# Attention values kept in rows of 4 KB and loaded earlier, with queries and keys ahead of them, more products ahead and more buffers

## The chip, the cores and the metric

One Trainium2 chip, one of its cores. The metric is the device time of one execution in microseconds (us); before the change the median of three runs is 1877.93 us (1871.57 to 1879.18).

## What is computed

One layer of a hybrid encoder on 1024 tokens of width 1024, in float32. Only branch A matters here:

```python
p = h @ w_in                       # h: normed, modulated x; q, k, v are 1024 columns each
q, k = rmsnorm(q, g_q), rmsnorm(k, g_k)      # per head, 16 heads of 64
z = q @ k.T / 8                    # strictly causal: s < t
log_a = log_sigmoid(z) + (exclusive suffix sum of log_sigmoid(-z))
y_a = (exp(log_a), 0 where s >= t) @ v
merged = sigmoid(ga) * (y_a @ w_a) + sigmoid(gb) * (y_b @ w_b)
```

With c[s] the product of sigmoid(-z) from s up to t, each weight is a difference of neighbouring c's. The kernel therefore scans sigmoid(-z) into c and multiplies c by dv, the differences of neighbouring rows of v. The last row of each block of 128 (vlast) is added as a bias. So every head pair needs v twice: from row 0 and from row 1 of a DRAM array that has one row of zeros in front.

## The kernel before, in words

Float32 operands are split into a high and a low part, and each product is three matmuls. The stages in order of time:

- **Values and keys (to about 178 us).** The first 512 columns of v (`finish_v`, L401) and all of k (`finish_k`, L379) are projected, 8 token tiles each. A finished key tile is transposed on PE (L392), scaled and split on ACT (L395) and DVE (L396) into a tile `khl` with tag `vs`, 3 buffers, and stored by two DMAs of ACT's queue (L398). While the last keys finish, PE already runs the first products of the next stage (`first_two`, L484).
- **Gates, queries, convolution inputs (to about 571 us).** A seven-product scheme. The sums of weights (s3, s2_, s1, s4, L627 to L630) are formed by POOL and split by ACT (L466) and DVE.
- **Attention (about 569 to 1036 us).** `att_load` (L707) loads a head's q and k, two parts each, with six DMAs on SP's queue. `load_v` (L719) loads a pair's v twice, into `vb` (e = 0, the shifted rows) and `va` (e = 1), one buffer each. `att_dv` (L727) forms vb - va on DVE once for each pair and splits one head's half of it into `vt`. `load_vlast` and `turn_vlast` (L737, L744) read the last rows of the blocks into a tile `vl`, which has the tag of `va` and so takes turns with it in the same buffer, and transpose it on PE (L747). The steps s = 8h + i run over 16 heads and 8 query blocks: `att_scores` (z on PE L774 and L775, sigmoid on ACT L776, scan on DVE L780), two steps later `att_trans` (PE L795, ACT L798, DVE L799), and every second step `att_av` (PE L810 and L811 into one PSUM bank `o`; ACT L815, DVE L817 into `oy`, 2 buffers, stored by SP, L819).
- **Fillers** (`fillers`, L869) run on PE between the attention steps: the other 512 columns of v in two weight sets e of 8 products each (24 matmuls of 256 columns, L884 to L886; each product is two yields of 1.3 planned us), stored to `d_v[1 + e]` on SP's queue (L889), then two products of branch B. A ratio (L945) spreads them: HEAD = 10 yields go ahead of the attention, TAIL = 20 of the planned 208 us are held back for after it. HEAD is not counted in what the ratio spreads, so 195 planned us are left after HEAD, 188 of them run inside the attention and 7 behind it.
- Behind it come the projection of branch A, the output projection and the FFN, which the change does not touch.

Each engine and each DMA queue runs its instructions in one fixed order. A planner fixes that order when the program is built, from the order of the code, the priorities, the free buffers and its own planned times. `issue_after(x)` adds an edge only for instructions on the same engine as x, and no wait for x to end. SP runs ahead of the other engines until an instruction in its order has to wait for data or a buffer; whatever is queued behind that instruction waits too.

Of the kernel before, what the change touches and what calls it, by code (L numbers as in the profile page):

```python
# [8 lines left out]
F32 = mybir.dt.float32  # L9
F32R = mybir.dt.float32r  # L10
# [6 lines left out]
P = 128  # L17
T = 1024
D = 1024
KT = D // P  # L20
H = 16
DH = 64
# [6 lines left out]
def block_kernel(tc, x, x_t, cols, ada_1, ada_2, ada_row, w_q, w_kv, w_v1, w_cg, w_a, w_b, w_o, w_g, w_u, w_d, out):  # L29
    nc = tc.nc  # L30
# [3 lines left out]
    drp = st.enter_context(tc.tile_pool(name="drp", bufs=1, space=DRAM))  # L34
# [3 lines left out]
    def nm(s):  # L38
        uid[0] += 1
        return f"{s}_{uid[0]}"  # L40
# [24 lines left out]
    d_q = [drp.tile([KT, P, T], F32, name=f"d_q{e}") for e in range(2)]  # L65
    d_k = [drp.tile([KT, P, T], F32, name=f"d_k{e}") for e in range(2)]

    d_v = [drp.tile([T + 1, n], F32, name=f"d_v{n}_{e}") for e, n in enumerate((512, 256, 256))]
    d_yb = [[drp.tile([P, KT, 512], F32, name=f"d_yb{e}{n}") for n in range(2)] for e in range(2)]
    d_ya = [drp.tile([P, KT, 512], F32, name=f"d_ya{n}") for n in range(2)]  # L70
    d_sga = drp.tile([KT, P, T], F32, name="d_sga")
# [307 lines left out]
    def finish_k(ps, i, ch):  # L379
        sq = gw.tile([P, 512], F32, tag="wlo", bufs=GS, name=nm("qsq"))  # L380
        nc.scalar.activation(sq, ps, AF.Square)
        ss = ap.tile([P, 8], F32, tag="qss", bufs=3, name=nm("qss"))
        nc.vector.tensor_reduce(out=ss, in_=sq.rearrange("p (h d) -> p h d", d=DH), op=ALU.add, axis=AX.X)
        qn = ap.tile([P, 512], F32, tag="qn", bufs=2, name=nm("qn"))
        r = rstd_of(ss, 1.0 / DH, ap, 8)
        nc.vector.tensor_tensor(out=qn.rearrange("p (h d) -> p h d", d=DH),
                                in0=ps.rearrange("p (h d) -> p h d", d=DH),
                                in1=r.unsqueeze(2).broadcast_to([P, 8, DH]), op=ALU.mult)
        yield
        tr = ps_tr()  # L390
        for j in range(4):
            nc.tensor.transpose(tr[:, j * P:(j + 1) * P], qn[:, j * P:(j + 1) * P], ident)  # L392
        hl_ = ap.tile([P, 2, 512], F32R, tag="vs", bufs=3, name=nm("khl"))
        hi, lo = hl_[:, 0], hl_[:, 1]
        nc.scalar.activation(hi, tr, AF.Identity, scale=kgc)  # L395
        nc.vector.scalar_tensor_tensor(out=lo, in0=tr, scalar=kgc, in1=hi.bitcast(F32), op0=ALU.mult, op1=ALU.subtract)  # L396
        for e, t in ((0, hi), (1, lo)):
            nc.scalar.dma_start(d_k[e][4 * ch:4 * ch + 4, :, i * P:(i + 1) * P].rearrange("j p t -> p j t"),  # L398
                                t.rearrange("p (j t) -> p j t", j=4).bitcast(F32))

    def finish_v(ps, i):  # L401
        vs = ap.tile([P, 512], F32, tag=("vs", "qn")[i % 2], bufs=3 - i % 2, name=nm("vs"))
        if i % 2:
            nc.vector.tensor_copy(out=vs, in_=ps)
        else:
            nc.scalar.activation(vs, ps, AF.Copy)
        nc.scalar.dma_start(d_v[0][1 + i * P:1 + (i + 1) * P], vs)

    tails = []
    split_w(4)  # L410
# [6 lines left out]
            split_w(5 + i // 2)  # L417
    ends = in_order(i0)
    for e in range(3):
        nc.scalar.dma_start(d_v[e][0:1], mk[0:1, :d_v[e].shape[1]])  # L420

    def more():

# [295 lines left out]
    def load_v(h, e):  # L719

        pr = h // 2
        d, c0 = (d_v[0], pr * P) if h < 8 else (d_v[1 + (h - 8) // 4], pr % 2 * P)
        t_ = ("vb", "va")[e]
        vab[t_] = bp.tile([P, KT, P], F32, tag=t_, bufs=1, name=nm(t_))
        lastld[0] = nc.sync.dma_start(vab[t_], d[e:T + e, c0:c0 + P].rearrange("(i p) d -> p i d", p=P))

    def att_dv(h):  # L727

# [7 lines left out]

    def load_vlast(e):  # L737

        vl = bp.tile([8, 512], F32, tag="va", bufs=1, name=nm("vl"))
        for d, c in (((0, 0),), ((1, 0), (2, 256)))[e]:  # L740
            nc.sync.dma_start(vl[:, c:c + d_v[d].shape[1]], d_v[d][1:].rearrange("(i p) d -> i p d", p=P)[:, P - 1])
        return vl

    def turn_vlast(e, vl):  # L744
# [6 lines left out]
    hd, vts, vab = {}, {}, {}  # L751
# [51 lines left out]
    def att_av(h, g):  # L803
        pr, e0 = h // 2, (h % 2) * DH
        vt = vts[h]
        o = pps.tile([P, 256], F32, tag="o", bufs=1, name=nm("o"))
        for j in range(2 * g + 2):
            c0 = P if j == 2 * g + 1 else 0
            th, tl = ats[h, g, j // 4]
            nc.tensor.matmul(o[:, c0:], vt[:, j, :], th[:, j % 4, c0:], start=(j == 0), stop=False)  # L810
            lastav[0] = nc.tensor.matmul(o[:, c0:], vt[:, j, :], tl[:, j % 4, c0:], start=False, stop=(j == 2 * g + 1))  # L811
        tmp = bp.tile([DH, 256], F32, tag="otmp", bufs=1, name=nm("otmp"))
        yv = bp.tile([DH, 256], F32, tag="oy", bufs=2, name=nm("oy"))
        for e in range(2):
            nc.scalar.activation(tmp[:, e * P:(e + 1) * P], o[:DH, e * P:(e + 1) * P], AF.Identity,  # L815
                                 bias=vlast[:, h, 2 * g + e:2 * g + e + 1])
        nc.vector.tensor_tensor(out=yv, in0=o[DH:], in1=tmp, op=ALU.add)  # L817
        hf, c0 = g // 2, (g % 2) * 256
        nc.sync.dma_start(d_ya[hf][e0:e0 + DH, pr, c0:c0 + 256], yv)  # L819
        yield (2 * g + 2) * 0.22  # L820
# [5 lines left out]
    def attention():  # L826

        steps = [(h, i) for h in range(H) for i in (LAST if h == H - 1 else ORDER)]
        for s in range(len(steps) + DAV):
            if s < len(steps):  # L830
                h, i = steps[s]
                if s % 8 == (0 if h else 3) and h + 1 < H:
                    with tc.issue_after(lastld[0].ins):
                        att_load(h + 1)
                if s % 16 in (10, 11) and h + 1 < H:
                    with tc.issue_after(lastz[0].ins):
                        load_v(h + 1, 11 - s % 16)
                if s % 8 == (6 if h % 2 else 5) and h + 1 < H:
                    att_dv(h + 1)
                if s == 54:  # L840
                    with tc.issue_after(lastld[0].ins):
                        vl = load_vlast(1)
                if s == 56:
                    turn_vlast(1, vl)
                yield from att_scores(h, i)
            if s >= DAV:
                h, i = steps[s - DAV]
                if s % 2 != DAV % 2:
                    yield from att_av(h, i // 2)
            if 0 <= s - 2 < len(steps):  # L850
                yield from att_trans(*steps[s - 2])
# [17 lines left out]
    def fillers():  # L869
        for e in range(2):  # L870
# [5 lines left out]
            for i in range(8):  # L876
# [9 lines left out]
                    nc.tensor.matmul(ps, sl, wh, start=False, stop=(k == KT - 1))  # L886
                vs = fq.tile([P, 256], F32, tag=("ybh", "ybl")[i % 2], bufs=2, name=nm("vs1"))
                nc.scalar.activation(vs, ps, AF.Copy)
                nc.sync.dma_start(d_v[1 + e][1 + i * P:1 + (i + 1) * P], vs)  # L889
                yield 1.3  # L890
        cb_w = {}
        for m, n in [(m, n) for m in range(KT - 2) for n in range(2)] + [(m, n) for n in range(2) for m in (KT - 2, KT - 1)]:
# [45 lines left out]

    FILL = 2.5 * 16 * 5.2
    ATT = sum((i + 1) * 0.2175 + (i % 2) * (i + 1) * 0.22 for i in range(8)) * H  # L940
    HEAD, TAIL = 10, 20.0
    fl = fillers()
    ta = tf = 0.0
    ratio = (FILL - TAIL) / ATT
# [9 lines left out]
    with tc.high_priority():  # L954
        vl = load_vlast(0)
        turn_vlast(0, vl)
        load_v(0, 1)
        load_v(0, 0)
        att_load(0)
        att_dv(0)  # L960
        for j in range(HEAD):
            next(fl)
    at_ = attention()
# [590 lines left out]
```

## Time and profile before

| | before |
|---|---|
| runs | 1879.18, 1871.57, 1877.93 us; median 1877.93 |
| profiled execution | 1873.62 us, its span 1871.8 us |
| PE busy | 1816.8 us, 97% of the span |
| DVE busy | 1355.4 us, 72% |
| ACT busy | 795.4 us, 42% |
| mean granted clock of PE | 0.992 |
| DMA issued by SP | 251.87 MB, 41.2% of the 16 engines' span |

The span runs from the first instruction to the last. Busy time is the time in which an engine had an instruction in work; PE's matmuls overlap, so its busy time says where it had nothing to do, not how fast it was. A clock of 1.00 is TensorE's upper level (2.4 GHz), 0.50 the lower (1.2 GHz). In a timeline, the bracket at the end of a row gives the idle time ahead of that instruction on its engine and who ended it.

### The profile page before, as it was taken

The page shows a single profiled execution, that of the slowest core. Times are in us where ns is not written, and L with a number is a line of the kernel's source. Part 1 is how long each engine was busy: PE and PEld are TensorE (multiplying, and loading weights), DVE is VectorE, ACT ScalarE, POOL GpSimd, SP SyncE. Part 2 cuts the span into 40 slices and gives each one's busy share as a digit, 9 for nine tenths or more (in the row PEclk, how much of TensorE's full clock was granted, in tenths as well). Part 3 has the DMA queues.
Part 4 walks back from the last instruction along what each step waited for, and adds up shares of the span by engine and source line. Part 5 has one row for each costly group of instructions (what it writes and reads, how often), then busy time and mean ns, then how long its engine had stood idle before and what let it go on. Part 6 is the DMA issues. An engine that isn't in the chain of part 4 may idle for free.

```text
span 1871.8 us, 24807 instructions
## 1 busy us (share of the span) xinstructions
PE 1816.8 (97%) x8829; PEld 1508.1 (81%) x8829; DVE 1355.4 (72%) x1950; ACT 795.4 (42%) x1488; POOL 373.5 (20%) x277
## 2 busy tenths in 40 slices
PE   7999999999998999999999999989999999999999
PEld 4787778888888988887888888867888888878887
DVE  6873877779964888786888544489877788744676
ACT  4342553333343656555556321554444334422321
POOL 1043328323320000000000000105544454300000
PEclk9999999999999999999999999999999999999999
DMA  9588451227738476678563636314443334389866
GB/s 389 197 307 310 160 177 68 85 89 248 279 135 268 126 192 164 186 182 293 153 161 123 212 116 216 136 59 166 164 174 135 146 146 170 123 308 334 291 228 221
DMA packets 156272, 357.45 MB, mean 191 GB/s; under 512 B 15451, under 2 KB 54637, under 8 KB 153974
## 3 DMA queue, kind: packets, MB, share of 16 engines
q1 hardware_dynamic: 103824, 251.87, 41.2%
q10 hardware_dynamic: 51318, 100.34, 14.6%
q0 software_dynamic: 1008, 3.67, 0.5%
q8 instruction: 70, 1.15, 0.3%
q14 instruction: 52, 0.43, 0.1%
HBM read 245.19 MB, written 110.63 MB: 190 GB/s over the span
## 4 chain that ended last, share of the span: by engine, by line
PE 77%; DVE 9%; DMA 6%; issue 4%; ACT 2%; POOL 0%; SPq 0%; ACTq 0%; DVEq 0%; POOLq 0%
PE e L127 6%; PE e L128 6%; PE e L129 6%; PE pj L127 5%; PE pj L128 5%; PE pj L129 5%; PE pj L290 5%; PE e L1381 4%; PE e L1382 4%; PE pj L865 4%; PE e L1383 4%; PE pj L866 4%; PE pj L867 4%; PE tr L795 3%; PE o L811 2%
## 5 line engine op out<-in xcount | busy, mean ns | idle before, releaser
L780 DVE TENSOR_TENSOR_SCAN pt<-pt,mk 128x128 f32<-128x128 f32 (+7 forms) x128 | 172.1, 1350 | 31.9 <-ACT pt L776 31.4
L776 ACT ACTIVATE pt<-z,rq 128x512 f32<-128x512 f32 (+2 forms) x192 | 108.0, 580 | 96.3 <-PE z L775 63.4
L127 PE MATMUL e<-big,whi 128*128 128x512 f32 x352 | 138.1, 392 | 3.9 <-ACT c L1282 2.5
L128 PE MATMUL e<-big,whi 128*128 128x512 f32 x352 | 137.7, 391 | 0.8 <-DVE big L132 0.8
L129 PE MATMUL e<-big,wlo 128*128 128x512 f32 x352 | 137.4, 390 | 0.0
L118 POOL TENSOR_SCALAR rs_m<-ss 128x1 f32<-128x1 f32 x8 | 2.4, 304 | 674.9 <-ACT xn L1197 674.9
L132 DVE TENSOR_TENSOR c<-e,c 128x512 f32<-128x512 f32 x142 | 95.4, 687 | 51.1 <-PE e L129 48.6
L127 PE MATMUL pj<-big,whi 128*128 128x512 f32 x320 | 125.1, 391 | 0.4 <-DVE c L132 0.4
L128 PE MATMUL pj<-big,whi 128*128 128x512 f32 x320 | 124.7, 390 | 0.0
L129 PE MATMUL pj<-big,wlo 128*128 128x512 f32 x320 | 124.3, 390 | 0.0
L1381 PE MATMUL e<-whi,f 128*128 128x512 f32 (+1 forms) x319 | 121.7, 382 | 1.3 <-DVE wt L132 1.3
L1382 PE MATMUL e<-wlo,f 128*128 128x512 f32 (+1 forms) x319 | 121.8, 382 | 0.0
L1383 PE MATMUL e<-whi,f 128*128 128x512 f32 (+1 forms) x319 | 121.6, 382 | 0.0
L132 DVE TENSOR_TENSOR c<-pj,c 128x512 f32<-128x512 f32 x140 | 93.3, 683 | 35.6 <-PE pj L129 35.3
L290 PE MATMUL pj<-whi,big 128*128 128x512 f32 x352 | 109.9, 398 | 4.0 <-ACT big L273 4.0
L132 DVE TENSOR_TENSOR wlo<-raw,whi 128x512 fp32r<-128x512 f32 x116 | 90.7, 785 | 30.7 <-ACT whi L466 30.7
L132 POOL TENSOR_TENSOR ws<-raw,raw 128x512 f32<-128x512 f32 x40 | 57.1, 1427 | 276.5 <-DMA raw<-w_cg 150.7
L799 DVE TENSOR_TENSOR atl<-tr,ath 128x512 fp32r<-128x512 f32 (+1 forms) x192 | 100.1, 549 | 16.2 <-ACT ath L798 14.7
L466 ACT ACTIVATE whi<-raw 128x512 fp32r<-128x512 f32 x116 | 72.3, 629 | 92.8 <-PE pj L128 40.7
L798 ACT ACTIVATE ath<-tr 128x512 fp32r<-128x512 f32 (+1 forms) x192 | 86.4, 489 | 46.0 <-PE o L810 25.0
L865 PE MATMUL pj<-big,whi 128*128 128x512 f32 x256 | 104.7, 409 | 0.0
L795 PE MATMUL tr<-dm,pt 128*128 128x128 f32 x576 | 96.0, 274 | 8.7 <-DVE atl L799 8.4
(254 smaller groups left out, 5041.3 us busy)
## 6 DMA issues: line engine op xcount, KB each, us to landing
f<-d_f SPq DMA_DIRECT2D x77, 512.0 KB, 4.2
d_f<-fs ACTq DMA_DIRECT2D x70, 512.0 KB, 3.4
raw<-w_cg SPq DMA_DIRECT2D x40, 512.0 KB, 3.7
raw<-w_g SPq DMA_DIRECT2D x25, 512.0 KB, 3.5
raw<-w_u SPq DMA_DIRECT2D x25, 512.0 KB, 3.3
ad<-ada ACTq DMA_DIRECT2D x19, 512.0 KB, 4.9
ada<-ada SPq DMA_DIRECT2D x8, 1024.0 KB, 9.3
d_t<-ts SPq DMA_DIRECT2D x16, 512.0 KB, 5.7
```

The costliest lines, as they stand in the source:

```text
L127: nc.tensor.matmul(ps, wh[:, k, :], fh[:, k, :], start=(k == 0), stop=False)
L128: nc.tensor.matmul(ps, wh[:, k, :], fl[:, k, :], start=False, stop=False)
L129: nc.tensor.matmul(ps, wl[:, k, :], fh[:, k, :], start=False, stop=(k == 3))
L132: eng.tensor_tensor(out=out, in0=a, in1=b, op=op)
L290: nc.tensor.matmul(ps, a, b, start=(k == 0 and q == 0), stop=(k == KT - 1 and q == 2))
L776: nc.scalar.activation(pt[:, off + s0:off + s0 + m], z[:, :m], AF.Sigmoid, scale=rq[:, 1, i, h:h + 1])
L780: nc.vector.tensor_tensor_scan(out=pt[:, rev], data0=pt[:, rev], data1=mk[:, rev], initial=1.0, op0=ALU.mult, op1=ALU.max)
L795: nc.tensor.transpose(tr[:, j * P:(j + 1) * P], pt[:, off + (b0 + j) * P:off + (b0 + j + 1) * P], ident)
L865: nc.tensor.matmul(ps, wh, rh_, start=(k == 0), stop=False)
L1381: nc.tensor.matmul(o, sh, w[0][:, c], start=(j == 0), stop=False)
L1382: nc.tensor.matmul(o, sh, w[1][:, c], start=False, stop=False)
L1383: nc.tensor.matmul(o, sl, w[0][:, c], start=False, stop=(j == NJ - 1))
```

## The change

- v goes to DRAM as rows of 4 KB: `d_v[pair][p]` holds, for one of 128 row positions p, the 128 columns of all 8 blocks. A load of a pair is 128 rows of 4 KB where it was 1024 pieces of 512 B. Stores into it become pieces of 512 B (they were 2 KB or 1 KB). The shifted version's position 0 is filled by a small copy inside DRAM, `put_before`, on SP's queue, once for each of the three arrays.
- `att_load(0)` is traced ahead of the two `load_v` of the first pair; `att_dv(0)` moves into step 2.
- `load_v` is traced at steps 7 and 8 of 16, for the next pair, where it was at steps 10 and 11.
- `vl` gets a buffer of its own.
- HEAD goes from 10 to 16 yields (5 to 8 products), and FILL now leaves HEAD out: 187.2 planned us are left after it, 177.2 inside the attention, TAIL = 10 behind it.
- `oy` has 3 buffers (2), the tag `vs` of the key parts 4 (3).

```diff
-    d_v = [drp.tile([T + 1, n], F32, name=f"d_v{n}_{e}") for e, n in enumerate((512, 256, 256))]
+    d_v = [drp.tile([n, P + 1, KT, P], F32, name=f"d_v{n}_{e}") for e, n in enumerate((4, 2, 2))]
...
-        hl_ = ap.tile([P, 2, 512], F32R, tag="vs", bufs=3, name=nm("khl"))
+        hl_ = ap.tile([P, 2, 512], F32R, tag="vs", bufs=4, name=nm("khl"))
...
-        vs = ap.tile([P, 512], F32, tag=("vs", "qn")[i % 2], bufs=3 - i % 2, name=nm("vs"))
+        vs = ap.tile([P, 512], F32, tag=("vs", "qn")[i % 2], bufs=4 - i % 2 * 2, name=nm("vs"))
...
-        nc.scalar.dma_start(d_v[0][1 + i * P:1 + (i + 1) * P], vs)
+        nc.scalar.dma_start(d_v[0][:, 1:, i].rearrange("r p d -> p r d"), vs.rearrange("p (r d) -> p r d", d=P))
...
+    def put_before(e):
+
+        nc.sync.dma_start(d_v[e][:, 0, 1:], d_v[e][:, P, :KT - 1])
+
+    put_before(0)
...
-        d, c0 = (d_v[0], pr * P) if h < 8 else (d_v[1 + (h - 8) // 4], pr % 2 * P)
+        d = d_v[0][pr] if h < 8 else d_v[1 + (h - 8) // 4][pr % 2]
...
-        lastld[0] = nc.sync.dma_start(vab[t_], d[e:T + e, c0:c0 + P].rearrange("(i p) d -> p i d", p=P))
+        lastld[0] = nc.sync.dma_start(vab[t_], d[e:P + e])
...
-        vl = bp.tile([8, 512], F32, tag="va", bufs=1, name=nm("vl"))
+        vl = bp.tile([8, 512], F32, tag="vl", bufs=1, name=nm("vl"))
...
-        yv = bp.tile([DH, 256], F32, tag="oy", bufs=2, name=nm("oy"))
+        yv = bp.tile([DH, 256], F32, tag="oy", bufs=3, name=nm("oy"))
...
-                if s % 16 in (10, 11) and h + 1 < H:
+                if s % 16 in (7, 8) and 16 * (s // 16) < 8 * H - 16:
                     with tc.issue_after(lastz[0].ins):
-                        load_v(h + 1, 11 - s % 16)
+                        load_v(2 * (s // 16) + 2, 8 - s % 16)
+                if s == 2:
+                    att_dv(0)
...
-                nc.sync.dma_start(d_v[1 + e][1 + i * P:1 + (i + 1) * P], vs)
+                nc.sync.dma_start(d_v[1 + e][:, 1:, i].rearrange("r p d -> p r d"), vs.rearrange("p (r d) -> p r d", d=P))
+                if i == 7:
+                    put_before(1 + e)
...
-    HEAD, TAIL = 10, 20.0
+    HEAD, TAIL = 16, 10.0
+    FILL -= 1.3 * HEAD
...
+        att_load(0)
         load_v(0, 1)
         load_v(0, 0)
-        att_load(0)
-        att_dv(0)
         for j in range(HEAD):
             next(fl)
```

## Rows read from the trace of the kernel before

**Rows 1.** The page's busy times, first engine.

```profile
PE 1816.8 (97%) x8829; PEld 1508.1 (81%) x8829; DVE 1355.4 (72%) x1950; ACT 795.4 (42%) x1488; POOL 373.5 (20%) x277
```

**Rows 2.** Busy by stretch: length, PE, PEld, DVE, ACT, POOL; clock, DMA share, GB/s.

```profile
600.00:1050.00 450.00, 434.67 (x2665) 379.07 (x2665) 370.88 (x513) 268.17 (x611) 0.00 (x0) 1.00 0.64 181
610.00:620.00 10.00, 10.00 (x83) 9.76 (x82) 9.91 (x15) 8.20 (x19) 0.00 (x0) 1.00 0.71 158
...
1010.00:1020.00 10.00, 10.00 (x53) 8.30 (x53) 9.56 (x12) 6.13 (x15) 0.00 (x0) 1.00 0.03 8
...
593.30:597.80 4.50, 4.49 (x20) 4.29 (x20) 1.12 (x2) 1.01 (x3) 0.00 (x0) 0.51 1.08 383
870.50:874.30 3.80, 3.74 (x17) 3.57 (x18) 2.82 (x5) 1.77 (x6) 0.00 (x0) 0.55 0.99 362
182.00:188.20 6.20, 6.13 (x15) 4.82 (x16) 2.64 (x5) 1.58 (x4) 0.12 (x1) 0.51 0.76 267
```

**Rows 3.** Timeline of SP's DMA issues where the attention begins: start, length, instruction.

```profile
568.88 0.40 SPq L725 DMA_DIRECT2D vb<-d_v  x1
569.50 7.32 SPq L714 DMA_DIRECT2D sqt<-d_q  x3
...
579.66 0.38 SPq L725 DMA_DIRECT2D va<-d_v  x1
...
592.37 1.16 SPq L455 DMA_DIRECT2D raw<-w_v  x2
```

**Rows 4.** Timeline of PE: first and last filler ahead of the attention, first score.

```profile
572.68 0.36 PE L884 MATMUL pj<-whi,big 128*128 128x256 f32 x1
...
587.57 0.28 PE L886 MATMUL pj<-whi,big 128*128 128x256 f32 x1
593.32 0.77 PE L774 MATMUL z<-skh,sqt 128*128 128x128 f32 x2 [5.47 <-DMA skh<-d_k]
```

**Rows 5.** Timeline of DVE and PE around 870 us.

```profile
869.99 0.43 DVE L817 TENSOR_TENSOR oy<-o,otmp 64x256 f32<-64x256 f32 x1 [4.10 <-DMA d_ya<-oy]
...
870.56 0.36 PE L810 MATMUL o<-ath,vt 128*128 128x256 f32 x1 [3.03 <-DVE oy L817]
```

**Rows 6.** Timeline of PE, SP and DVE, 777 to 787 us.

```profile
777.47 0.19 PE L747 MATMUL tr<-dm,vl 8*64 8x8 f32 x1
...
777.69 0.37 SPq L725 DMA_DIRECT2D va<-d_v  x1
...
784.90 1.23 DVE L132 TENSOR_TENSOR vb<-vb,va 128x1024 f32<-128x1024 f32 x1 [4.28 <-DMA va<-d_v]
...
786.91 0.33 PE L795 MATMUL tr<-dm,pt 128*128 128x128 f32 x1 [2.61 <-DVE atl L799]
```

**Rows 7.** Timeline of PE, ACT and POOL at the end of the keys.

```profile
176.37 0.60 PE L392 MATMUL tr<-dm,qn 128*128 128x128 f32 x4
...
182.07 0.80 PE L127 MATMUL pj<-ft,whi 128*128 128x512 f32 x1 [3.25 <-ACT whi L466]
...
177.00 0.69 ACT L395 ACTIVATE khl<-tr,cst 128x512 fp32r<-128x512 f32 x1 [7.04 <-DMA d_k<-khl]
...
176.43 1.28 POOL L132 TENSOR_TENSOR ws<-raw 128x512 f32<-128x512 f32 x1
```

**Rows 8.** Timeline of DVE and SP near 655 us, one of five like it.

```profile
654.62 0.68 DVE L132 TENSOR_TENSOR vt<-vb,vt 128x512 fp32r<-128x512 f32 x1
...
655.33 0.37 SPq L725 DMA_DIRECT2D vb<-d_v  x1
```

**Rows 9.** Waits of whole tile vb: engine waited for, us, times.

```profile
  DMA vb<-d_v: 10.6, 5
```

**Rows 10.** DMA issues, whole span: queue, count, KB each, median us to landing.

```profile
raw<-w_g SPq DMA_DIRECT2D x25, 512.0 KB, 3.5
...
d_k<-khl ACTq DMA_DIRECT2D x32, 256.0 KB, 6.5
...
vb<-d_v SPq DMA_DIRECT2D x8, 512.0 KB, 4.5
```

More of the change, by code (lines that the diff above doesn't have):

```diff
@@ L419, in block_kernel @@
     for e in range(3):
-        nc.scalar.dma_start(d_v[e][0:1], mk[0:1, :d_v[e].shape[1]])
+        n = d_v[e].shape[0]
+        nc.scalar.dma_start(d_v[e][:, 0:1, 0].rearrange("r p d -> p r d"), mk[0:1, :n * P].rearrange("p (r d) -> p r d", d=P))
+    def put_before(e):
+        nc.sync.dma_start(d_v[e][:, 0, 1:], d_v[e][:, P, :KT - 1])
+    put_before(0)
     def more():
@@ L737, in load_vlast @@
     def load_vlast(e):
-        vl = bp.tile([8, 512], F32, tag="va", bufs=1, name=nm("vl"))
+        vl = bp.tile([8, 512], F32, tag="vl", bufs=1, name=nm("vl"))
         for d, c in (((0, 0),), ((1, 0), (2, 256)))[e]:
-            nc.sync.dma_start(vl[:, c:c + d_v[d].shape[1]], d_v[d][1:].rearrange("(i p) d -> i p d", p=P)[:, P - 1])
+            n = d_v[d].shape[0]
+            nc.sync.dma_start(vl[:, c:c + n * P].rearrange("i (r d) -> i r d", d=P), d_v[d][:, P].rearrange("r i d -> i r d"))
         return vl
```

## The prediction

> **What bounds it now.** The page comes first: PE is busy 97% of the span [rows 1], so only about 55 us of PE idle time are there to be had, plus what PE loses at the lower clock. The busy times by stretch say how little of that lies in the attention: PE idles 15.3 us of the 450 between 600 and 1050 us, while DVE idles 79.1 [rows 2]. PE is the bound there, and DVE comes close in places: 12 of those 45 slices of 10 us have DVE at 95% or more, of which the first and the last are shown [rows 2]. A timeline of PE then gives the holes. Four of them touch names of this change, and behind three PE runs at half its clock for a while.
>
> - At 587.85 PE has done its fillers and waits 5.47 us for keys [rows 4]; then 4.5 us at clock 0.51 [rows 2].
> - At 870.56 it waits 3.03 us for DVE, which waits to write `oy` until an older `oy` has been stored [rows 5]; then 3.8 us at 0.55 [rows 2].
> - At 786.91 it waits 2.61 us, behind a DVE that stood 4.28 us for `va` [rows 6].
> - At 182.07 it waits 3.25 us for a weight part that ACT was late with [rows 7]; then 6.2 us at 0.51 [rows 2].
>
> **The change, part by part.**
>
> *The head: queries and keys first, HEAD 16.* SP issued one value load ahead of the first query, was held 7 us within the first queries, and put the other value load among the keys [rows 3]. That one needed the buffer of `vl`, which has its own now. With all six loads of head 0 in front, the keys come no later than now, at 593.3. The hold itself stays: it lies in the row of the queries, not of the values. The three more products follow the last filler at its pace: five took from 572.68 to 587.85 [rows 4], about 3.0 us each, so PE has work until 596.8, 3.5 us past the moment at which the keys are there now. The hole closes: 5.47 us, and with it (1 - 0.51) x 4.5 = 2.2 us of clock. **Gain 7.7**, ends 0 (the hole moves) and 7.7. The work of the three products is moved, not added. If that cover is gone, z is again what PE waits for.
>
> What is late next: the fillers behind HEAD need the second weight set, whose two loads went out at 592.37 [rows 3]. A 512 KB weight load lands in 3.5 us at best [rows 10], so at about 597, and must then be split by ACT and DVE, while before the remaining three products of the first set bridged this time. PE has short attention steps to do meanwhile. **Cost 1.5**, a fifth of the present hole, between 0 and the whole 7.7 again; nearer to 0 because landing (597) and need (596.8) nearly meet.
>
> *`oy` with three buffers.* The wait of 4.10 us on DVE [rows 5] is for the store of the tile before last; with one more buffer it is for a store one product older, which is over. PE gets back 3.03 and (1 - 0.55) x 3.8 = 1.7. **Gain 4.7**, ends 0 and 4.7.
>
> *`vl` apart from `va`.* SP issued the `va` load 0.03 us after PE's last transpose of `vl` had ended [rows 6]. Without the shared buffer it goes out as soon as the pair before has been subtracted. **Gain 2.6**, ends 0 and 2.61.
>
> *Seven steps ahead.* I count nothing for it. Of the five waits for `vb` (10.6 us of DVE together [rows 9]), the row is the same each time: the load is issued 0.03 us after DVE has read the old `vb` for the odd head [rows 8]. The buffer sets the time, not the step in the code; one buffer stays, and issue_after on a PE instruction gives SP no edge. Ends: 0 and 2.0, which is 10.6 times the rate of the next paragraph.
>
> *Rows of 4 KB.* Equal sizes: 512 KB in 512 B pieces land in 4.5 us, 512 KB in 4 KB rows in 3.5 [rows 10]. Five waits shorter by 1.0 make 5.0 us of DVE. PE feels DVE's idle time at the rate 15.3 / 79.1 = 0.19 [rows 2]. **Gain 1.0**, ends 0 and 5.0. Against it speaks the Trainium skill (DMA: Bandwidth & Descriptors, Specifications), by which pieces of 512 B already move at line rate. By that rule this term is 0 and the sum 1.0 smaller; the row, which mixes stages of different load, does not exclude it.
>
> *Stores in 512 B pieces.* The nearest row is a key store of 256 KB in such pieces, 6.5 us [rows 10]. The eight of `finish_v` lie beside a PE without a gap until 178 us, with key weights already loaded; the sixteen of the fillers hold nothing but their own buffers. **0**; if that cover is gone, one store time, 6.5.
>
> *`put_before`, three times on SP.* Each waits for the store just ahead and holds SP up to 6.5 us [rows 10]; behind it stand `d_ya` stores (one more buffer now) and the next weights, which are loaded about a product ahead. The first stands before the attention, where SP's weight loads have tens of us of slack. **0**; its price is in the slow rival.
>
> *`att_dv(0)` in step 2.* DVE's 1.23 us, as the same operation took at 784.90 [rows 6], and the split move behind two short scans. Values are issued at most six queue slots later and PE's first use is step 4. **0**; if values come late the scans queue behind, ends 0 and 4.28 as at 784.90.
>
> *A fourth key part.* Two things end at 177.0 together: PE's transposes (176.97) and the store ACT is said to have waited for [rows 7]. The buffer removes one. If the planner, no longer short of a buffer, lets the transposes go earlier, ACT can split the sum that POOL finished at 177.71 [rows 7] before PE runs dry at 178.8, worth 3.25 + (1 - 0.51) x 6.2 = 6.3. If not, 0. **Gain 3.1**, the middle, for nothing in the trace decides.
>
> *A thinner attention.* 188 - 177.2 = 10.8 planned us of filler leave it: 7.8 to the head, 3 to the tail, where they run as PE work. In the 12 of 45 slices that DVE fills, taking PE work away shortens nothing: **cost** 10.8 x 12/45 = **2.9**, ends 0 and 10.8.
>
> **Sum.** 7.7 - 1.5 + 4.7 + 2.6 + 1.0 + 3.1 - 2.9 = 14.7 us off. The profiled execution took 1873.62, so 1858.9 against it. It lies 4.3 under the median of the three runs; the four times together have the mean 1875.6, so I forecast **1861 us**. Under 0.5% (9.4 us) a difference can't be told from none.
>
> **Rivals.**
>
> *Holes that move.* The head's hole reappears at the second weight set, and the transposes stay late. For: both loads compete with head 1's keys on a DMA that is full there (share 1.08 [rows 2]). Against: SP is no longer held at `va`. 14.7 - 6.2 - 3.1 = 5.4 off: 1870. Chance 0.22.
>
> *All of it lands.* Key end in full, no loss at the second set, DVE absorbs the thinner attention. For: 79 us of DVE idle. 14.7 + 3.2 + 1.5 + 2.9 = 22.3 off: 1853. Chance 0.13.
>
> *Slower: SP held by `put_before`.* The copy waits for a store just issued, and PE needs the weights queued behind. Two copies lie in the attention: 2 x 6.5 us of PE, and as much clock in proportion as at the head (7.7 / 5.47): 18.3 us against 14.7 gained: 1879. It decides once the copy stands ahead of the next weight load in SP's order and that load is needed within 6.5 us. Against: weights go out well ahead, and SP often stands waiting with PE busy. Chance 0.07.
>
> The forecast has the remaining 0.58.
>
> **How the numbers follow.** Its own range is the sum with the half-open terms at their ends (keys 3.1 either way, thinning 2.9, run to run 4, which will not all fall on one side: 8 of their 10): 1853 to 1869. To leave out 2 in 10 the range goes to the second rival's centre and past the first's: **1851 to 1873**. Faster than 1868.5: nine tenths of the forecast, a quarter of the first rival, all of the second: 0.70, taken as 0.68 for the order of instructions that may shift elsewhere. Slower by over 0.5%: half of the third plus the same unknown, 0.06. Same: 0.26.
>
> **What would show it.** Right: no idle time over 1 us ahead of the first L774, and clock 1.00 there; no L817 that waits for `d_ya`; `va` loads right after the subtraction of the pair before; `vb` loads still just behind `vt`. The key end is open: an L127 without a wait, or with 3 us. Wrong: a wait of PE for L466 soon after the first scores; DVE filling more than 20 of the 45 slices; SP waiting for `d_v` stores with PE idle behind it.

## The result, and the profile after

The changed kernel takes **1881.8 us** (median of 15 executions, 1876.55 to 1887.89) beside 1874.83 us of the kernel before (15 executions): a ratio of **1.0037, interval 1.0024 to 1.0049**. That is 7 us slower, inside the 0.5% that counts as no change, and outside the forecast range, whose upper end was 1873 us. I forecast 14 us the other way.

The profiled execution has a span of 1879.1 us, against 1871.8 before. To see where the time went I cut both at the first filler product and at the first product of branch A's projection. The stretch between them is called the attention below, the one behind it the rest. These are the busy times of both stretches after the change (columns: stretch, its length, then busy time and count of PE, PEld, DVE, ACT and POOL, granted clock, DMA share, GB/s):

```profile
572.39:1040.88 468.49, 448.41 (x2771) 393.50 (x2770) 371.47 (x511) 270.62 (x620) 0.00 (x0) 0.98 0.62 183
1040.88:1879.10 838.22, 820.56 (x3638) 676.43 (x3636) 568.52 (x818) 299.31 (x497) 181.80 (x139) 0.99 0.51 184
```

And these, in the same columns, of the kernel before:

```profile
572.68:1036.69 464.01, 443.21 (x2772) 389.26 (x2770) 367.80 (x508) 269.23 (x618) 0.00 (x0) 0.99 0.65 184
1036.69:1871.80 835.11, 818.13 (x3638) 674.26 (x3636) 571.03 (x822) 300.70 (x500) 184.27 (x139) 1.00 0.51 185
```

The head starts at the same time. The attention is 4.5 us longer and the rest, whose code is untouched, 3.1. In the attention PE idles 468.49 - 448.41 = 20.1 us, against 20.8 before. So the holes that the change was meant to close have been replaced by others of the same size, and PE's busy time rose by 5.2 us for the same work, which fits the lower clock (0.98 for 0.99) behind the new holes.

The rows that the forecast named for the head, `oy` and `va` did change as it said. The first score follows the fillers without a hole, where [rows 4] show 5.47 us. No DVE instruction waits for a store of `oy` any more [rows 5]. The next `va` goes out 0.02 us after the subtraction of the pair before [rows 6] (775.22 below). The end of the keys hardly moved: 2.32 us for 3.25 [rows 7]. From the timeline of PE in the changed kernel:

```profile
181.01 0.50 PE L127 MATMUL pj<-ft,whi 128*128 128x512 f32 x1 [2.32 <-ACT whi L473]
...
583.80 0.40 PE L782 MATMUL z<-skh,sqt 128*128 128x128 f32 x2
```

What is new stands on SP. This is its timeline while the fourth pair runs; the values are those of the fifth (start, length, instruction):

```profile
762.14 0.47 SPq L722 DMA_DIRECT2D skh<-d_k  x1
762.70 0.55 SPq L721 DMA_DIRECT2D sqt<-d_q  x1
763.30 0.59 SPq L723 DMA_DIRECT2D skl<-d_k  x1
763.94 0.59 SPq L721 DMA_DIRECT2D sqt<-d_q  x1
764.57 0.59 SPq L722 DMA_DIRECT2D skh<-d_k  x1
765.21 0.59 SPq L723 DMA_DIRECT2D skl<-d_k  x1
765.91 0.53 SPq L732 DMA_DIRECT2D vb<-d_v  x1
...
775.22 0.32 SPq L732 DMA_DIRECT2D va<-d_v  x1
```

The `vb` load stands behind all six query and key loads of the next head. Its buffer was free earlier, when DVE had read the old `vb` (the `vt` row below ends at 763.53). It goes out 2.4 us after that and shares the DMA with six transfers of 256 KB: it is subtracted 8.1 us after its issue, and the DMA engines are 90% busy between 762 and 774 us. In the same way the next three go out 6.1, 3.0 and 3.0 us after their buffer is free. In the kernel before that gap was 0.03 us [rows 8]. Ahead of the six, SP had waited for a key buffer, but it was let go at 762.14, before the buffer of `vb` was free, and so it was for the next three. What delays the issue of `vb` is therefore the time in which SP issues the six, some 0.6 us each, in the second case with gaps of 0.8 to 1.4 us ahead of four of them. The timelines of DVE and PE of the changed kernel show what follows at 774 and at 836 us:

```profile
762.84 0.69 DVE L132 TENSOR_TENSOR vt<-vb,vt 128x512 fp32r<-128x512 f32 x1
...
773.97 1.23 DVE L132 TENSOR_TENSOR vb<-vb,va 128x1024 f32<-128x1024 f32 x1 [3.13 <-DMA vb<-d_v]
...
836.09 1.23 DVE L132 TENSOR_TENSOR vb<-vb,va 128x1024 f32<-128x1024 f32 x1 [3.03 <-DMA vb<-d_v]
...
777.21 0.48 PE L782 MATMUL z<-skh,sqt 128*128 128x128 f32 x1 [2.65 <-ACT pt L784]
...
837.92 0.36 PE L818 MATMUL o<-ath,vt 128*128 128x256 f32 x1 [1.13 <-DVE oy L825]
...
843.26 0.44 PE L803 MATMUL tr<-dm,pt 128*128 128x128 f32 x2 [1.49 <-DVE atl L807]
```

DVE stands 3 us for `vb`, its scans come late, and PE runs dry behind it. And the clock falls, as it did behind the old holes [rows 2]. Two stretches behind new holes, the second at the end of the attention behind a hole of 2.92 us that comes long after the last `vb` load (columns as above):

```profile
777.50:781.00 3.50, 3.50 (x12) 2.81 (x11) 2.11 (x4) 1.38 (x5) 0.00 (x0) 0.50 0.81 265
...
1026.90:1031.00 4.10, 3.98 (x17) 3.91 (x18) 1.41 (x3) 1.47 (x3) 0.00 (x0) 0.50 0.81 263
```

DVE's waits for `vb` add up to more than before [rows 9]; 11.0 us of them belong to the last four pairs, which before had 8.0. From the waits of the changed kernel (us in total, times, longest):

```profile
DVE vb L132 <- DMA vb<-d_v: 15.6, 7, 3.1
```

In the rest, the largest growth is one hole of PE, 3.94 us where the kernel before has 2.46 in front of the same product. The first fence is of the changed kernel, the second of the one before; each shows the row of PE and then ACT's order around the copy that PE waited for:

```profile
1299.97 0.80 PE L127 MATMUL e<-big,whi 128*128 128x512 f32 x1 [3.94 <-ACT c L1294]
...
1297.70 0.63 ACT L1068 ACTIVATE whi<-raw 128x512 fp32r<-128x512 f32 x1 [2.13 <-DVE fs L132]
...
1299.32 0.60 ACT L1294 ACTIVATE c<-e 128x512 f32<-128x512 f32 x1 [0.99 <-DVE fs L132]
```

```profile
1295.04 0.50 PE L127 MATMUL e<-big,whi 128*128 128x512 f32 x1 [2.46 <-ACT c L1282]
...
1294.41 0.58 ACT L1282 ACTIVATE c<-e 128x512 f32<-128x512 f32 x1
1294.89 0.62 ACT L1056 ACTIVATE whi<-raw 128x512 fp32r<-128x512 f32 x1
```

The planner has put a weight split, which waits for DVE, ahead of that copy. No line of this code was changed. The hole alone is 1.5 us longer; behind it PE also runs at the lower clock, which it did not before. The first row is of the changed kernel, the second of the one before (columns as above):

```profile
1300.00:1305.00 5.00, 5.00 (x12) 3.94 (x13) 4.93 (x9) 2.74 (x6) 0.00 (x0) 0.50 0.87 295
```

```profile
1295.00:1300.00 5.00, 4.96 (x22) 4.11 (x23) 4.93 (x8) 2.12 (x4) 1.62 (x1) 1.00 0.69 249
```

### The profile page after: what moved, and what is told of

Same layout as the page of the kernel before. It is cut to its first block, busy times and chain, and to the rows that moved or that the text cites. A ratio compares the mean times of both kernels' runs of the same rounds, so it can differ in the third digit from the quotient of the medians.

```text
span 1879.1 us, 24810 instructions
## 1 busy us (share of the span) xinstructions
PE 1824.8 (97%) x8829; PEld 1514.4 (81%) x8829; DVE 1355.7 (72%) x1950; ACT 795.7 (42%) x1488; POOL 370.3 (20%) x277
## 3 DMA queue, kind: packets, MB, share of 16 engines
q10 hardware_dynamic: 54400, 100.34, 14.7%
## 5 line engine op out<-in xcount | busy, mean ns | idle before, releaser
L784 ACT ACTIVATE pt<-z,rq 128x512 f32<-128x512 f32 (+3 forms) x192 | 107.2, 579 | 86.1 <-PE z L783 54.7
```

What stands on the lines that cost most here:

```text
L784: nc.scalar.activation(pt[:, off + s0:off + s0 + m], z[:, :m], AF.Sigmoid, scale=rq[:, 1, i, h:h + 1])
```

## The experiments

Three theories stood at the start. **A:** the new loss is the `vb` load queued behind six others. **B:** the attention, with fewer fillers, is too thin to cover DVE. **C:** a shifted order in the feed-forward. All runs in one table; attention and rest are the two stretches above in one profiled execution each, so a single value there carries some us of run to run (the profiled executions of e8, e9 and e12 are the fastest of their runs, that of e7 the slowest), and the ratio decides.

| kernel | median, us | ratio to before [interval] | attention | rest |
|---|---|---|---|---|
| before | 1874.83 | 1 | 464.0 | 835.1 |
| changed | 1881.80 | 1.0037 [1.0024, 1.0049] | 468.5 | 838.2 |
| e1: values first | 1866.57 | 0.9951 [0.9935, 0.9967] | 450.7 | 837.5 |
| e17: the same again | 1865.04 | 0.9949 [0.9930, 0.9968] | 448.6 | 840.9 |
| e2: HEAD 10 | 1867.12 | 0.9952 [0.9932, 0.9972] | 456.6 | 838.6 |
| e9: values first, HEAD 10 | 1867.34 | 0.9955 [0.9938, 0.9972] | 444.4 | 839.4 |
| e16: six first, HEAD 10 | 1881.20 | 1.0033 [1.0019, 1.0047] | 468.0 | 838.2 |
| e4: values at step 10 | 1868.85 | 0.9968 [0.9953, 0.9983] | 456.3 | 837.9 |
| e8: before + head | 1876.78 | 1.0014 [0.9995, 1.0033] | 462.0 | 837.5 |
| e12: before + seven steps | 1880.43 | 1.0013 [0.9998, 1.0027] | 460.1 | 837.1 |
| e15: before + head + seven steps | 1883.98 | 1.0035 [1.0019, 1.0052] | 474.0 | 835.1 |
| e3: before + rows of 4 KB | 1877.35 | 1.0007 [0.9989, 1.0024] | 464.6 | 834.7 |
| e10: values first, old rows | 1865.27 | 0.9952 [0.9935, 0.9969] | 452.7 | 837.9 |
| e7: before + `oy` 3 + own `vl` | 1870.35 | 0.9985 [0.9963, 1.0006] | 470.2 | 834.7 |
| e13: values first, three key parts | 1864.80 | 0.9928 [0.9911, 0.9946] | 448.8 | 841.3 |
| e18: the same again | 1863.75 | 0.9940 [0.9923, 0.9956] | 449.5 | 840.2 |
| e14: values first, early split | 1863.84 | 0.9925 [0.9905, 0.9945] | 450.9 | 838.0 |
| e19: both | 1862.70 | 0.9935 [0.9917, 0.9953] | 449.9 | 837.9 |

**Values first (e1).** In each step the block with the value loads is moved ahead of the block with the queries and keys, whose `issue_after` then keeps them behind the values on SP:

```diff
+                if s % 16 in (7, 8) and 16 * (s // 16) < 8 * H - 16:
+                    with tc.issue_after(lastz[0].ins):
+                        load_v(2 * (s // 16) + 2, 8 - s % 16)
                 if s % 8 == (0 if h else 3) and h + 1 < H:
                     with tc.issue_after(lastld[0].ins):
                         att_load(h + 1)
-                if s % 16 in (7, 8) and 16 * (s // 16) < 8 * H - 16:
-                    with tc.issue_after(lastz[0].ins):
-                        load_v(2 * (s // 16) + 2, 8 - s % 16)
```

> The changed kernel with the value block written ahead of the query and key block in each attention step, nothing else: SP then sends the even heads' values before the six query and key loads of that step instead of behind them. Theory A (the give-back is the value load queued behind six loads): the last four vb loads land in about 4 us instead of 6.6 to 7.2, DVE's waits for vb fall from 15.6 us to under 9, the PE holes that follow them (777, 838 to 843, 945) close or shrink, and the time falls by 5 to 10 us, to 0.995 to 0.998 of the kernel before. Theory B (the six more products taken out of the attention leave it too thin): waits for vb may fall, but PE goes idle elsewhere in the attention and the time stays within 2 us of the changed kernel, 1.003 to 1.004. Theory C (the loss is a shifted order in the feed-forward, where the code is the same): the time from 1253 to 1657 us of the kernel before, which grew by 4.0, stays long and the whole falls by 3 us at most.

Measured: 0.9951, 9 us faster than before and 15 faster than the changed kernel (1881.80 - 1866.57; 16 by the ratios), more than A expected. SP's and DVE's timelines at the sixth pair of values first, `vb` now ahead of the six:

```profile
871.83 0.32 SPq L732 DMA_DIRECT2D vb<-d_v  x1
872.24 0.47 SPq L721 DMA_DIRECT2D sqt<-d_q  x1
872.76 0.59 SPq L722 DMA_DIRECT2D skh<-d_k  x1
...
876.03 1.20 DVE L132 TENSOR_TENSOR vb<-vb,va 128x1024 f32<-128x1024 f32 x1
```

No bracket stands behind the subtraction: DVE has no idle time there, and the same holds for all of the last four pairs. Not all of this is the load: with the new order the planner also placed each of these four subtractions one or two scans earlier in DVE's own order. The two stretches, in the columns of before:

```profile
578.06:1028.77 450.71, 440.46 (x2771) 389.03 (x2770) 369.84 (x511) 270.06 (x621) 0.00 (x0) 0.99 0.65 191
1028.77:1866.30 837.53, 819.30 (x3638) 675.73 (x3636) 568.72 (x819) 298.99 (x497) 180.47 (x139) 0.99 0.52 184
```

PE's idle time in the attention halves, 20.1 to 10.3 us, and its busy time for the same work falls by 8.0, most of it the clock that had been lost. What SP itself stands for tells the same. The first fence is the list of waits of SP in the changed kernel, the second in values first (line waited for: us, times, longest):

```profile
SPq L722 <- PE z L783: 35.2, 10, 8.6
SPq L732 <- DVE vt L132: 11.1, 2, 6.5
```

```profile
SPq L732 <- DVE vt L132: 37.0, 6, 8.0
SPq L722 <- PE z L783: 10.4, 5, 8.6
```

In the changed kernel SP mostly stood at a key load, waiting for PE to free the key buffer, with `vb` queued behind it. Those waits cost `vb` nothing by themselves, since they ended before its own buffer was free; the six issues behind them did. In values first SP stands at `vb` itself, so this load goes out the moment its buffer is free.

**HEAD and TAIL back (e2).**

```diff
-    HEAD, TAIL = 16, 10.0
-    FILL -= 1.3 * HEAD
+    HEAD, TAIL = 10, 20.0
```

> The changed kernel with HEAD and TAIL back at 10 and 20 and FILL as before, nothing else. Theory A: the planner then puts most vb loads ahead of the six query and key loads again, though not all, so the waits for vb fall by about half; but the hole of the head returns (about 5 us and 2 of clock): within 4 us of the changed kernel, 1.000 to 1.004. Theory B: the attention is as thick as before, the holes tied to DVE go, and with the oy and va holes gone too the time is below the kernel before: 0.994 to 0.998. Theory C: as with A for the attention, and the feed-forward stretch gets back to within 1 us of before or stays 4 us longer independent of the waits for vb.

Measured: 0.9952, as B had it. But the planner also puts the last four `vb` loads ahead of the six here, so the run does not tell A from B. Nor did the head's hole return, as I had expected: the order of the head's loads alone closes it. The profile has waits for `vb` of 15.7 us in sum, as many as the changed kernel, 7.05 of them in one wait at 880 us, behind loads of weights and of branch B. Behind that one PE idles 3.44 us. Their sum is thus no measure by itself; what counts is where PE runs dry behind them. The next two runs separate the theories.

**Values first with HEAD 10 (e9).** The edits of e1 and e2 together.

> Values first (as in the first run) and HEAD 10, TAIL 20, FILL as before on top: the value loads stand ahead of the six others here too, so this tells the price of the thinner attention by itself. Theory A: no gain left in thickness, and the hole at the head is closed already by the order of its loads: within 3 us of values first, 1864 to 1870. Theory B (thin attention costs, my term 2.9, ends 0 and 10.8): 3 to 10 us faster than values first, 1856 to 1863.

Measured: 0.9955, against 0.9951 with HEAD 16. The thinner attention costs nothing that can be measured once `vb` is ahead; the two intervals are too wide to exclude the 2.9 us of my term. One of the 12 executions took 3657.52 us, and nothing here explains it; without it the median would be 1866.64.

**All six first with HEAD 10 (e16).** On e2, each `vb` load is issued only behind the last key load of the next head:

```diff
-            nc.sync.dma_start(skl[es].bitcast(F32), d_k[1][pr, e0:e0 + DH, :])
+            lastk[0] = nc.sync.dma_start(skl[es].bitcast(F32), d_k[1][pr, e0:e0 + DH, :])
...
-                    with tc.issue_after(lastz[0].ins):
+                    with tc.issue_after((lastk if s % 16 == 8 else lastz)[0].ins):
                         load_v(2 * (s // 16) + 2, 8 - s % 16)
```

> The changed kernel with HEAD 10, TAIL 20 and FILL as before, and a wait in SP's order that puts every vb load behind all six query and key loads; the run with the same HEAD and vb ahead measured 0.9952. Theory A (the order on SP is the cause by itself): the waits for vb come back with PE holes behind them, 8 to 16 us slower than vb ahead: 1.000 to 1.004. Theory A with B (late vb costs only where the attention is thin): the thicker attention covers the waits, within 4 us of vb ahead: 0.994 to 0.997.

Measured: 1.0033, 14 us over e2 (1881.20 - 1867.12). So the order on SP costs time without a thin attention too. Timelines of DVE and PE in this run:

```profile
841.11 1.22 DVE L132 TENSOR_TENSOR vb<-vb,va 128x1024 f32<-128x1024 f32 x1 [5.99 <-DMA vb<-d_v]
...
844.11 1.33 PE L804 MATMUL tr<-dm,pt 128*128 128x128 f32 x5 [5.19 <-DVE atl L808]
```

Part of this price isn't the late four: the edit holds the earlier pairs too. A hole of 4.49 us for a weight split at 620 us and one of 2.31 at 671 are new in it, beside 1.75, 5.19 and 1.25 us behind the late four (at 784, 844 and 951). How much of the 14 us falls to the late four is not shown.

**Values back at steps 10 and 11 (e4).** Only the two lines of the condition and the call go back. In SP's order the late `vb` then stands behind two of the six.

> The changed kernel with the value loads back at steps 10 and 11, nothing else; in SP's order the last four vb loads then stand behind two of the next head's six query and key loads, where the changed kernel has them behind six and the kernel with values first behind none. Theory A (what stands ahead of vb on SP): between the two, the waits for vb at about half of 11 us, time 1868 to 1877. Theory B (the thinner attention) sees no reason for a difference from the changed kernel: 1879 to 1884. A rival to A, that the step in the code matters for its own sake: as the kernel before, waits of 10 us, 1872 to 1877, which A can't be told from by the time alone but by the waits.

Measured: 0.9968, between behind none (0.9951) and behind six (1.0037), near the first. The last four waits for `vb` sum to 5.1 us where the changed kernel has 11.0, the half that theory A asked for. The rival asked for waits of 10 us and 1872 to 1877; all waits sum to 10.4, but the time lies below its range, so the step for its own sake does not explain it. The interval overlaps that of values first.

**The head alone (e8).** On the kernel before: `att_load(0)` first, `att_dv(0)` in step 2, HEAD 16, TAIL 10, FILL less HEAD.

> The kernel before with the order of the head's loads, HEAD 16, TAIL 10, the smaller FILL and the later split alone; layout, buffers and the steps of the value loads as before (vl still shares a buffer with va). My prediction's terms: the head's hole closes (7.7), the second weight set costs 1.5, the thinner attention 2.9: 3.3 us faster, 0.998. Theory B: the attention is longer by 8 us or more and the whole is slower than before: 1.002 to 1.005. Theory A: the attention loses no more than 3 us and the whole is 0.996 to 1.000, since the vb loads stand behind two of the six others and not behind all.

Measured: 1.0014, an interval that holds 1 and touches neither 0.998 nor a loss of 8 us. The attention of its profile is 2.1 us shorter, near the 3.3 of my terms, but the rest is 2.4 longer: theory C's shift. The last four `vb` stand behind two of the six.

**Seven steps ahead alone (e12), and both (e15).** On the kernel before: the two lines of the step, alone and on top of e8.

> The kernel before with the value loads seven steps ahead alone, at steps 7 and 8. HEAD is 10, and in SP's order the vb loads still stand ahead of the six query and key loads. My prediction: 0 (0 to 2.0 faster). Theory A: the step costs nothing as long as the order on SP stays, 0.998 to 1.001, waits for vb as before (10 us). Rival (the earlier step costs by itself): 1.002 or more.

> The kernel before with two parts of the change together: the head's group as in the run of the head alone, and the value loads seven steps ahead. Each part alone keeps vb ahead of the six (seven steps) or behind two of them (head alone); the two together put three of the late vb loads behind all six, with rows of 512 B. Theory A: waits for vb over 14 us, PE holes behind them as in the changed kernel, 4 to 10 us slower than the head alone: 1.003 to 1.007 of the kernel before. Theory B or a step without weight: as the head alone, 1.000 to 1.003. Theory C: in the feed-forward ACT's copy of the product stands ahead of the next weight split here, as in the kernel before and unlike in the changed one; then the stretch from the first product of ya to the end is 834 to 836 us as in the kernel before, not 837.5 or more.

Measured: 1.0013 alone, where the last four `vb` stay ahead of the six: nothing that can be told from 1, as forecast, but its interval does not exclude the rival's 1.002 either. One earlier load, at 716.45 us, does stand behind all six in this run, and its subtraction comes 7.5 us later, after 2.56 us of waiting. With the head: 1.0035, 4 us over the head alone (0.0021 of 1875), though the two intervals overlap. Neither part moves one of the last four `vb` behind all six by itself; together they do, for the last three pairs. By the times alone the two parts simply add up (0.0013 + 0.0014 against 0.0035); that the pair does more than its parts is seen in the order on SP. The profile of both has the longest attention of all, and its rest is that of the kernel before. Its stretches, then its row of the hole in the rest:

```profile
573.09:1047.07 473.98, 452.35 (x2771) 397.14 (x2770) 371.44 (x511) 271.05 (x620) 0.00 (x0) 0.97 0.65 181
1047.07:1882.20 835.13, 819.41 (x3638) 675.36 (x3636) 568.57 (x818) 298.83 (x497) 183.48 (x139) 0.99 0.53 185
```

```profile
1305.08 0.50 PE L127 MATMUL e<-big,whi 128*128 128x512 f32 x1 [1.46 <-ACT c L1284]
```

That is theory C's part told apart: here ACT's copy stands ahead of the weight split again. Over all profiles the hole is 0.92 to 2.46 us in the five kernels with the copy ahead (before, e3, e7, e12, e15) and 3.00 to 4.36 in the other thirteen. The rest is 834.7 to 837.1 us long in the five and 837.5 to 841.3 in the thirteen, some 3 us apart. In e8 the shift came with the head's edits, which lie 700 us earlier; in e15 it went again with two lines more.

**Rows of 4 KB: alone (e3) and taken out (e10).** e3 has the kernel before with the new `d_v`, its stores and loads and the three copies; e10 has values first with the old ones.

> The kernel before with the new layout of the values alone (rows of 4 KB, stores in 512 B pieces, the three copies); order of the loads, HEAD, buffers as before. My prediction's terms: 1.0 us faster (0 to 5.0), copies 0. Theory A: vb still goes out ahead of the queries and keys and lands in 3.5 us instead of 4.5; 0 to 5 us faster, 0.997 to 1.000. A rival: rows of 4 KB move no faster when queries and keys share the queues, vb lands in 4.5 as before: 0.999 to 1.001. Theory that the copies or the stores cost: slower, over 1.002, with SP held at the copy and PE idle behind it.

> Values first with the old layout (rows of 512 B, stores in rows, no copies), all else as changed: the price of the 4 KB rows and the three copies once the loads stand in the right order. Rows alone on the kernel before gave 1.0007. If rows of 4 KB are what lets vb land in time here: waits for vb of 3 to 10 us come back and the time is 3 to 8 us over values first. If the order is all: within 2 us of values first, 1864 to 1869.

Measured: 1.0007, and 0.9952 against 0.9951. In the time the rows are worth nothing that can be measured either way, and the copies and stores cost nothing that can. In the old rows with values first, none of the last four subtractions waits for `vb` either.

Yet longer rows do land sooner. Where `vb` has the same neighbours in SP's order and DVE waits for it in both kernels, the last three subtractions come 4.2, 4.6 and 4.7 us after the issue in the kernel before and 3.6, 3.6 and 3.7 us in e3; all waits for `vb` sum to 7.8 us for 10.6. SP's and DVE's rows of the last pair, first of the kernel before, then of e3:

```profile
934.43 0.37 SPq L725 DMA_DIRECT2D vb<-d_v  x1
...
939.15 1.23 DVE L132 TENSOR_TENSOR vb<-vb,va 128x1024 f32<-128x1024 f32 x1 [2.97 <-DMA vb<-d_v]
```

```profile
942.61 0.32 SPq L732 DMA_DIRECT2D vb<-d_v  x1
...
946.27 1.23 DVE L132 TENSOR_TENSOR vb<-vb,va 128x1024 f32<-128x1024 f32 x1 [1.91 <-DMA vb<-d_v]
```

**`oy` and `vl` alone (e7).** On the kernel before, `bufs=3` for `oy` and a tag of its own for `vl`.

> The kernel before with three buffers for oy and a buffer of its own for vl, nothing else. My prediction's terms: oy 4.7 (0 to 4.7) and vl 2.6 (0 to 2.61), so 7.3 faster, 0.996. Rival: the waits close but PE's holes reappear at the next wait of DVE for vb, which comes sooner: 0 to 3 us faster, 0.9985 to 1.000.

Measured: 0.9985, 2.8 us, an interval that holds 1. Its profile, an execution 13 us over its median, shows one thing to mind. With a buffer of its own `vl` no longer holds back `va`, so both value loads now go out ahead of the first queries, and the head's hole doubles. SP's timeline, then PE's:

```profile
573.21 0.40 SPq L725 DMA_DIRECT2D va<-d_v  x1
573.71 0.51 SPq L725 DMA_DIRECT2D vb<-d_v  x1
574.36 8.82 SPq L714 DMA_DIRECT2D sqt<-d_q  x3
```

```profile
603.27 0.80 PE L774 MATMUL z<-skh,sqt 128*128 128x128 f32 x2 [11.10 <-DMA raw<-w_v]
```

**The fourth key part and the later split (e13, e14, then e17, e18, e19).** e13 is values first with three buffers of the tag `vs`; e14 is values first with `att_dv(0)` back ahead of the fillers; e19 has both edits.

> Values first without the fourth key part (three buffers, stores of values on them as before). My prediction's term for it: 3.1 (0 to 6.3), so 3 us over values first: 1869 to 1871, the hole at 182 back at 3.2 us and 6.2 us at half clock behind it. Rival, by the changed kernel's trace, where PE had won 1 us at 182 and only 0.3 at 519: within 2 us of values first, 1865 to 1868.

> Values first with the first split of the values back ahead of the fillers instead of in step 2. My prediction: the move costs 0 (0 to 4.28 if the scans queue behind it). In the changed kernel DVE waited 2.64 us for vb there, with no idle time of PE behind it: within 2 us of values first, 1865 to 1869. If DVE, now waiting for the values ahead of the first scans, makes PE wait: 3 to 5 us more, 1869 to 1872.

Both came out 4 to 5 us under e1, which no theory asked for. So values first and e13 ran again, beside a kernel with both:

> Values first once more, the same kernel as in the first run, beside the next two. If the difference to the runs without the fourth key part or with the early split was the session: 0.992 to 0.9935. If those parts cost something: 0.9945 to 0.996 again.

> Values first without the fourth key part, again: 0.9918 to 0.994 as before; whether it lies under values first beside it by more than 0.15% tells if the fourth part costs.

> Values first without the fourth key part and with the early first split, both: if each is worth 4 to 5 us by itself, 0.990; if both differences were the session, as values first beside it, within 0.15%.

Measured side by side: 0.9949, 0.9940 and 0.9935, with intervals of 0.0016 to 0.0019 to either side. Neither the fourth part nor the later split gains anything; whether they cost 1 to 3 us stays open. The fastest kernel measured, by medians, is e19 with 1862.70 us; against values first the intervals don't separate it. Every kernel with values first beats both the kernel before and the changed one.

## Why the prediction was wrong

The step that failed is **"Seven steps ahead. I count nothing for it"**, with its reason "The buffer sets the time, not the step in the code". The buffer does set the time as long as `vb` is what SP stands at, and the sign that the prediction named ("`vb` loads still just behind `vt`") is the one that did not hold: for the last four pairs the load came 2.4 to 6.1 us behind `vt`. The step in the code, with the thinner attention of HEAD 16, changed what stands ahead of `vb` in SP's order. The planner put six loads ahead. SP spends some 0.6 us on the issue of each before it comes to `vb`, and beside them `vb` then takes 7.0 to 9.0 us to its subtraction, where e9, with the same rows of 4 KB and `vb` ahead, has three at 3.4 to 3.6; no run separates these two parts of the delay. Shown by e1, whose edit undoes nothing but this order and takes 15 us off, and from the other side, less cleanly, by e16. I priced the parts one by one. Alone, e12 and e8 cost nothing that can be told from nothing, and neither puts one of the last four `vb` behind all six.

Point by point:

- **Head, +7.7:** the hole closed, in every run with the new order of loads, HEAD 10 or 16. What that is worth by itself no run shows. The cost of 1.5 at the second weight set did not appear: in the changed kernel PE has no idle time over 0.4 us between 584 and 700 us. That e8 as a whole gains nothing lies, by its one profile, in the rest and in `vb`.
- **`oy`, +4.7, and `vl`, +2.6:** both waits are gone in the changed kernel (in e2 one for a store of `oy`, 1.68 us, is back). Alone on the kernel before they gave 2.8 of 7.3 (0.9985, an interval that holds 1); the head's hole that grew there, where the order of the first loads was the old one, is seen in the one profile, the slowest execution.
- **Rows, +1.0:** nothing in the time (e3 1.0007, e10 0.9952 against 0.9951), but intervals of 0.0016 to 0.0018 to either side can't tell 1 us from 0. By the Trainium skill (DMA: Bandwidth & Descriptors, Specifications) pieces of 512 B already move at line rate, and the prediction's alternative by that rule was 0. The times agree with it; the rows of e3 do not, where the load is used 0.6 to 1.1 us sooner in rows of 4 KB. So the premise of the term, waits shorter by about 1 us, was right.
- **Stores, copies, `att_dv(0)`, 0:** right within the noise. SP was held at the copies for 7.9 us in two waits, and no idle time of PE follows. With rows of 512 B and the later split PE does idle 1.3 to 2.1 us for a scan at 591 to 593 us, behind late first values (e8, e10, e15): inside the term's range of 0 to 4.28, where it was put at 0. The slower rival had the right kind of mechanism, a load held behind something on SP, and the wrong instruction.
- **Fourth key part, +3.1:** 0. A hole of 2.3 to 2.6 us stands at 181 to 183 us in the other seventeen profiles, with three buffers and with four; the 3.25 of [rows 7] was one execution's.
- **Thinner attention, -2.9:** 0 within the noise (e9 against e1).
- **Not in the sum:** the rest, about -3, from an order that the planner changed some 250 us behind the last edited work.

With the order on SP put right, and the rows, the key part, the thinner attention and the second weight set at 0, the terms give 14.7 - 1.0 - 3.1 + 2.9 + 1.5 - 3 = 12.0 us; values first measured 9.2 (interval 6.2 to 12.2). So what is left of the sum is not refuted, though 12.0 lies near the edge and its terms are not confirmed one by one. Of the 21 us between forecast and result (1881.8 - 1861), 15 are the one order on SP and about 3 the rest.

## What to carry to other kernels

On a queue that issues in order, the price of moving a load is not read from its own row, but from what it is placed behind and what those wait for: list the order of that queue around it after the change, and count for each load ahead how long its buffer holds it, how long its issue takes and how much of the transfer it shares. Where two loads compete, fix their order by hand (here three lines moved) so that the one whose consumer is already idle goes first. Parts that each leave a planned order nearly as it was can change it together, so one of the runs should have them in pairs; and a planner can move instructions far from any edit, so look at the untouched stretches as well.

## What the runs showed of the hardware

- Six loads of 256 KB issued ahead of one of 512 KB delay it well beyond their issue time: in the changed kernel the last four subtractions come 8.1, 9.0, 7.0 and 7.2 us after `vb` was issued, where before, issued ahead of them, three came 4.2 to 4.7 us after it, and in e9, ahead and in the same rows of 4 KB, three came 3.4 to 3.6 us after it. DVE waited for the load each time.
- The same load of 512 KB at the same place in SP's order was subtracted 4.2 to 4.7 us after its issue as 1024 pieces of 512 B (before) and 3.6 to 3.7 us after it as 128 rows of 4 KB (e3).
- The granted clock is 0.50 in the stretches shown behind holes of PE of 2.65 and 2.92 us, as behind the holes of before. In the attention of the changed kernel against values first, 9.8 us of idle time came with 8.0 us more busy time for the same work; in the kernel before against values first, 10.6 us of idle time came with 2.8. So a hole can cost nearly twice its length where the clock falls behind it, but not at a fixed rate.
